# Gate and up products of the last feed-forward as pairs of 64-row products

## The chip, the cores and the metric

The kernel runs on one core of one Trainium2 chip. The metric is the device time of one execution in microseconds (us), from two runs and one more execution that the hardware profiler recorded. Engines are named as in the profile: PE multiplies matrices (PEld is its weight load), DVE, ACT and POOL do elementwise work, SP issues the transfers between the chip's main memory and on-chip memory. Products land in PSUM, in eight banks of 128 partitions by 512 numbers.

## The reference

Two layers over 512 tokens of width 1024. Each layer has a mixer, an attention into 256 memory tokens and a feed-forward with a gate; each of the three is added to its input and normalised. The change is in the feed-forward of the second layer:

```python
FFN_HIDDEN = 2816
def post_norm(h, sub, g, b):
    return layer_norm(DEEPNORM_ALPHA * h.astype(jnp.float32) + sub.astype(jnp.float32), g, b).astype(h.dtype)
...
def swiglu(h, wg, wu, wd):
    return (jax.nn.silu(h @ wg) * (h @ wu)) @ wd
...
        h = post_norm(h, memory_cross_attention(h, mem, xq_w[layer], xk_w[layer], xv_w[layer], xo_w[layer]),
                      ln_x_g[layer], ln_x_b[layer])
        h = post_norm(h, swiglu(h, ffn_wg[layer], ffn_wu[layer], ffn_wd[layer]),
                      ln_ffn_g[layer], ln_ffn_b[layer])
```

## The kernel before

**Numbers in two parts.** Every float32 operand of a large product is split into `hi` (rounded to the format fp32r) and `lo` (the rest, also fp32r). `mm3` replaces one product by three that add up in one bank: hi by hi, hi by lo, lo by hi. An fp32r product of 128 rows, 128 weight columns and 512 moving columns is one PE instruction with one weight load.

**Weights.** `weights` loads a block of 512 KB into a `raw` buffer (two of them), ACT copies it to `hi`, DVE subtracts to get `lo` (four buffers each). Its priority is put 200 places ahead of its users, so loads run early. One block feeds 24 products of 512 columns.

**Order.** Nothing is issued directly. `Order.add` records every operation with the tiles it reads and writes. `Order.order` then plays the program through with a cost for each operation and gives each engine its sequence: the ready operation with the lowest program number goes first, if its buffers can be had. `together` records several products as one operation, so that nothing comes between them; they are issued from line 437, all else from line 439. On the chip each engine follows its sequence strictly.

**The feed-forward** (`ffn`). The hidden width of 2816 is done in two parts, 12 and 10 column blocks of 128 (`FFN_PARTS` counts pairs of them). In each part the gate and up products come first, with the hidden unit on the partitions and the 512 tokens on the moving side: for two blocks of 128 at a time, four banks (gate and up, two blocks), eight steps of 128 input features, three products each. `sink` turns a gate bank and an up bank into one hidden tile: tanh on ACT, two DVE operations, and the split into hi and lo. Then `gemm_tok` multiplies by `wd`, with the tokens on the partitions, in two halves of 512 output columns: four banks, one for each token tile of 128. All but the last eight feature steps are done for the four token tiles together, the last eight token tile by token tile, so that a token tile's end can be worked on while the next is multiplied.

**The input of the feed-forward** is `self.hT`, the normalised tokens turned to features on the partitions, in four tiles (`big_1839` to `big_1842` below, two feature steps each). The attention's output projection before it ends token tile by token tile; `norm_half` normalises a token tile on DVE, `block_to_feat` has PE turn 128 by 128 squares (products with `ident`), and `split` writes the hi part by ACT and the lo part by DVE. The first pair of column blocks (`early`) is done in two halves of 256 tokens, so that its first half needs two of the four token tiles only.

Of the kernel before, what the change touches and what calls it, by code (L numbers as in the profile page):

```python
# [12 lines left out]
AF = mybir.ActivationFunctionType  # L13
OP = mybir.AluOpType
AX = mybir.AxisListType

P = 128
# [443 lines left out]
class Trunk:  # L461
# [755 lines left out]
    def ffn(self, layer, after, fill=iter(())):  # L1217
        a = self.a
        V, A = self.o.V, self.o.A
        wg, wu, wd = a["ffn_wg"][layer], a["ffn_wu"][layer], a["ffn_wd"][layer]  # L1220
        _, _, hact, _ = self.feat_view(self.hT)
        g, b = self.norm_rows("ln_ffn_g", "ln_ffn_b", layer)
        for part, (b0, b1) in enumerate(FFN_PARTS):
            nm = (b1 - b0) * 2
            _, hat, _, htok = self.feat_view([self.big() for _ in range(nm // 2)])

            def sink(m, pg, pu):
                th, sg = self.t2(), self.t2()
                A.activation(th, pg, AF.Tanh, scale=0.5)
                V.scalar_tensor_tensor(sg, th, 1.0, pg, op0=OP.add, op1=OP.mult)  # L1230
                V.tensor_tensor(sg, sg, pu, op=OP.mult)
                self.split(hat(m)[:, 0], hat(m)[:, 1], sg)

            for cb in range(b0, b1):
                pss = [self.bank() for _ in range(4)]
                early = cb == 0
                ws = {}
                for hs in ([slice(0, S // 2), slice(S // 2, S)] if early else [slice(0, S)]):
                    for kh in range(2):
                        for n, w in enumerate((wg, wu)):  # L1240
                            if (kh, n) not in ws:
                                ws[kh, n] = self.weights(w, kh * 4, 4, cb * 256, 256)
                            hi, lo = ws[kh, n]
                            for k in range(4):
                                x = hact(kh * 4 + k)
                                for m in range(2):
                                    cs = slice(m * P, (m + 1) * P)
                                    self.mm3(pss[n * 2 + m][:, hs], (hi[:, k, cs], lo[:, k, cs]), (x[0][:, hs], x[1][:, hs]),
                                             kh == 0 and k == 0, kh == 1 and k == 3)
                for m in range(2):  # L1250
                    sink((cb - b0) * 2 + m, pss[m], pss[2 + m])
                next(fill, None)
            last = part == len(FFN_PARTS) - 1
            for half in range(2):
                rs = self.residual_sinks(half, 2 * ALPHA if part == 0 else 1.0, 4 * LN_EPS, g, b, last, after)
                self.gemm_tok(wd, b0 * 2, nm, half * 512, htok, NT, rs, tail=TAIL)
# [458 lines left out]
```

## Time and profile before

| | |
|---|---|
| median of 2 runs | 1542.75 us (1540.59 and 1544.91) |
| profiled execution | 1543.56 us, span of its instructions 1541.8 us |
| PE busy | 1508.7 us of the span, 8220 products |
| DVE, ACT busy | 984.9 us, 552.5 us |
| mean granted PE clock | 0.995 of 2.4 GHz |
| transfers | 184.01 MB, mean 119 GB/s |

The span runs from the first to the last instruction of the execution; the profiled execution took 1.8 us more than its span. A PE instruction's recorded duration is longer than its turn, since products are pipelined: the turn is read from the start of one to the start of the next.

### The profile page before, as it was taken

To read this page: it belongs to the slowest core of one execution; us is meant where nothing else is said; L and a number is where in the kernel's file an instruction comes from. 1 tells how busy PE (TensorE), PEld (TensorE's weight loads), DVE (VectorE), ACT (ScalarE), POOL (GpSimd) and SP (SyncE) were. 2 spreads that over 40 slices of the span, in tenths; PEclk is the share of its full clock that TensorE was granted. 3 is DMA by queue.
4 is the path that set the end of the run, shared out by engine and by line. 5 is a ranking of instruction groups with operands and counts; after the bars stand their busy time and mean duration, and the time that the engine had idled before them with its cause. 6 is when DMAs were issued, how large, how long until landed. Compare 5 with 4: busy or idle time off the path is not lost.

```text
span 1541.8 us, 21120 instructions
## 1 busy us (share of the span) xinstructions
PE 1508.7 (98%) x8220; PEld 1268.3 (82%) x8220; DVE 984.9 (64%) x1880; ACT 552.5 (36%) x1008; POOL 57.0 (4%) x97
## 2 busy tenths in 40 slices
PE   7999899999999999999999899999999999999998
PEld 5888788689889887888888898888889888888886
DVE  6986576697557888626845899647557444234436
ACT  5533346544523354324341333323423222122311
POOL 1100000010100000010000000000000000000000
PEclk9999999999999999999999999999999999999999
DMA  6424134235223355445562652333212333233322
GB/s 201 115 57 123 47 119 137 64 98 163 62 76 116 110 192 176 150 165 174 186 220 76 245 191 86 128 110 121 65 57 82 109 99 102 85 110 96 96 69 96
DMA packets 125396, 184.01 MB, mean 119 GB/s; under 512 B 14128, under 2 KB 84656, under 8 KB 121200
## 3 DMA queue, kind: packets, MB, share of 16 engines
q1 hardware_dynamic: 125296, 182.66, 37.6%
q8 instruction: 65, 1.06, 0.3%
q14 instruction: 35, 0.29, 0.1%
HBM read 162.45 MB, written 20.19 MB: 118 GB/s over the span
## 4 chain that ended last, share of the span: by engine, by line
PE 88%; DVE 7%; DMA 2%; ACT 1%; issue 1%; SPq 0%; POOL 0%; DVEq 0%; ACTq 0%; POOLq 0%
PE ps L439 86%; DVE t L439 4%; DVE big L439 2%; PE ps L437 2%; DVE lo L439 1%; DMA raw<-in_hyb_w_in_dram 1%; DVE tiny L439 0%; DMA big<-s5m 0%; ACT big L439 0%; DMA raw<-in_xo_w_dram 0%; ACT hi L439 0%; ACT t L439 0%; DMA posi<-in_pos_t_dram 0%; SPq L439 0%; ACT L439 0%
## 5 line engine op out<-in xcount | busy, mean ns | idle before, releaser
L439 PE MATMUL ps<-big,hi 128*128 128x512 f32 (+1 forms) x2368 | 649.5, 360 | 6.1 <-ACT hi L439 4.5
L439 PE MATMUL ps<-hi,big 128*128 128x512 f32 x1728 | 548.2, 394 | 0.7 <-ACT big L439 0.4
L439 PEld LDWEIGHTS ps<-big,hi 128*128 128x128 f32 x2368 | 420.7, 190 | 72.4 <-ACT hi L439 4.7
L439 ACT ACTIVATE hi<-raw 128x1024 fp32r<-128x1024 f32 (+2 forms) x252 | 263.5, 1046 | 513.7 <-PE ps L439 355.7
L439 DVE TENSOR_TENSOR lo<-raw,hi 128x1024 fp32r<-128x1024 f32 (+2 forms) x252 | 303.4, 1205 | 224.8 <-ACT hi L439 221.4
L439 PE MATMUL ps<-big,lo 128*128 128x512 f32 (+1 forms) x1184 | 423.7, 359 | 2.5 <-DVE lo L439 2.5
L439 PEld LDWEIGHTS ps<-hi,big 128*128 128x128 f32 x1728 | 322.6, 188 | 66.4 <-DVE big L439 0.9
L439 PE MATMUL ps<-lo,big 128*128 128x512 f32 x864 | 338.3, 393 | 1.0 <-DVE lo L439 1.0
L439 PEld LDWEIGHTS ps<-big,lo 128*128 128x128 f32 x1184 | 224.6, 190 | 34.5 <-DVE lo L439 2.9
L439 PEld LDWEIGHTS ps<-lo,big 128*128 128x128 f32 x864 | 162.4, 188 | 35.5 <-DVE lo L439 2.2
L439 ACT ACTIVATE big<-ps 128x256 fp32r<-128x256 f32 (+2 forms) x188 | 89.4, 508 | 211.1 <-PE ps L439 202.0
L439 ACT ACTIVATE t<-ps 128x512 f32<-128x512 f32 (+6 forms) x147 | 68.8, 485 | 147.7 <-PE ps L439 139.0
L439 DVE TENSOR_TENSOR big<-ps,big 128x256 fp32r<-128x256 f32 (+1 forms) x152 | 77.6, 541 | 56.9 <-ACT big L439 54.7
L439 DVE SCALAR_TENSOR_TENSOR big<-big,ps 128x512 f32<-128x512 f32 x56 | 38.4, 685 | 86.7 <-PE ps L439 86.7
L439 DVE SCALAR_TENSOR_TENSOR t<-t,ps 128x512 f32<-128x512 f32 x72 | 49.0, 682 | 68.5 <-ACT t L439 49.8
L439 ACT ACTIVATE big<-t 32x128 f32<-32x128 f32 (+2 forms) x148 | 64.9, 455 | 24.3 <-DVE t L439 19.9
L439 DVE SCALAR_TENSOR_TENSOR big<-big,tiny,t 128x512 f32<-128x512 f32 x96 | 66.6, 745 | 0.0
L439 PE MATMUL ps<-ident,t 128*128 128x128 f32 x344 | 62.7, 275 | 3.4 <-ACT t L439 1.8
L439 POOL TENSOR_TENSOR tiny<-tiny,mhalf 128x1 f32<-128x1 f32 (+1 forms) x28 | 23.1, 825 | 962.3 <-DVE tiny L439 953.6
L439 PEld LDWEIGHTS ps<-ident,t 128*128 128x128 f32 x344 | 42.5, 140 | 15.6 <-ACT t L439 5.1
L439 PE MATMUL ps<-big,big 128*128 128x256 f32 (+2 forms) x328 | 54.9, 314 | 0.0
L439 PEld LDWEIGHTS ps<-big,big 128*128 128x128 f32 x328 | 47.8, 190 | 5.0
(145 smaller groups left out, 929.4 us busy)
## 6 DMA issues: line engine op xcount, KB each, us to landing
raw<-in_ffn_wg_dram SPq DMA_DIRECT2D x44, 512.0 KB, 3.8
raw<-in_ffn_wu_dram SPq DMA_DIRECT2D x44, 512.0 KB, 3.6
raw<-in_ffn_wd_dram SPq DMA_DIRECT2D x44, 512.0 KB, 4.1
s5m<-big SPq DMA_DIRECT2D x16, 1024.0 KB, 4.2
big<-s5m SPq DMA_DIRECT2D x16, 1024.0 KB, 6.3
raw<-in_hyb_w_in_dram SPq DMA_DIRECT2D x26, 512.0 KB, 3.8
raw<-in_xk_w_dram SPq DMA_DIRECT2D x16, 512.0 KB, 3.6
raw<-in_xv_w_dram SPq DMA_DIRECT2D x16, 512.0 KB, 4.1
```

Of the source, the lines that this page charges most:

```text
L437: op.inst = getattr(self.eng[e], f)(*a, **k)
L439: op.inst = getattr(self.eng[e], fn)(*args, **kw)
```

## The change

In the second layer the gate and up products take one column block of 128 at a time. Each product of 128 rows becomes two of 64 rows, one in each half of the rows, recorded `together`, and each half adds up in a bank of its own. Behind them ACT copies the first bank of gate to a scratch tile and DVE adds the second bank to it; likewise for up; the two sums go to `sink`. A weight block now holds all eight feature steps of one column block (128 columns, in runs of 512 bytes) where it held four steps of two column blocks (256 columns, 1024 bytes). The number of blocks stays 44. The branch for `early` is no longer taken in this layer.

```diff
+            if layer:
+                for m in range(nm):
+                    pss = [[self.bank() for _ in range(2)] for _ in range(2)]
+                    for n, w in enumerate((wg, wu)):
+                        hi, lo = self.weights(w, 0, 8, (b0 * 2 + m) * P, P)
+                        for k in range(8):
+                            x = hact(k)
+                            for i, (l, r) in enumerate(((hi, x[0]), (hi, x[1]), (lo, x[0]))):
+                                self.o.together(0.227, [
+                                    ((pss[n][u], l[u * 64:(u + 1) * 64, k], r[u * 64:(u + 1) * 64]),
+                                     dict(start=k == 0 and i == 0, stop=k == 7 and i == 2)) for u in range(2)])
+                    sums = []
+                    for n in range(2):
+                        z = self.t2()
+                        A.activation(z, pss[n][0], AF.Copy)
+                        V.tensor_tensor(z, pss[n][1], z, op=OP.add)
+                        sums.append(z)
+                    sink(m, *sums)
-            for cb in range(b0, b1):
+            for cb in range(b0, b1) if not layer else ():
```

PE where the attention's output projection (`ps_1870` is its last bank) goes over into the feed-forward; `ps_1893` takes the turned squares of the last token tile. Before:

```order
L439 MATMUL ps_1870<-hi_1881,big_1758 128x512
L439 MATMUL ps_1905<-big_1839,hi_1910 128x256 x2
L439 MATMUL ps_1905<-big_1839,lo_1911 128x256
...
L439 MATMUL ps_1908<-big_1842,hi_1919 128x256 x2
L439 MATMUL ps_1908<-big_1842,lo_1920 128x256
L439 MATMUL ps_1893<-ident_72,big_1674 128x128 x4
L439 MATMUL ps_1894<-ident_72,big_1674 128x128 x4
```

Between the first and the last of these 256-column products stand 96 of them in all, with three groups of turned squares among them. After the change, the same place:

```order
L439 MATMUL ps_1870<-hi_1881,big_1758 128x512
L439 MATMUL ps_1888<-ident_72,big_1673 128x128 x4
L439 MATMUL ps_1890<-ident_72,big_1674 128x128 x4
L439 MATMUL ps_1891<-ident_72,big_1674 128x128 x4
L439 MATMUL ps_1893<-ident_72,big_1674 128x128 x4
L437 MATMUL ps_1905<-big_1839,hi_1910 128x512
L437 MATMUL ps_1906<-big_1839,hi_1910 128x512
L437 MATMUL ps_1907<-big_1839,hi_1913 128x512
L437 MATMUL ps_1908<-big_1839,hi_1913 128x512
L437 MATMUL ps_1919<-big_1839,hi_1924 128x512
L437 MATMUL ps_1920<-big_1839,hi_1924 128x512
```

The 96 products are gone from here: PE has the turned squares alone between the projection and the first pair, which stands behind `ps_1893`. The two products of a pair follow each other in two banks.

DVE at the same place, the last token tile (`tiny_1892`): the operations with `t_1766` and `t_1767` are the first of the two of its normalisation, those with `t_1768` and `t_1769` the second. Before:

```order
L439 SCALAR_TENSOR_TENSOR big_1674<-big_1674,tiny_1892,t_1766_1843 128x512
L439 SCALAR_TENSOR_TENSOR big_1674<-big_1674,tiny_1892,t_1767_1844 128x512
L439 TENSOR_TENSOR big_1841<-ps_1891,big_1841 128x2x128
L439 TENSOR_TENSOR big_1842<-ps_1891,big_1842 128x2x128
L439 SCALAR_TENSOR_TENSOR big_1674<-big_1674,tiny_1892,t_1768_1845 128x512
L439 SCALAR_TENSOR_TENSOR big_1674<-big_1674,tiny_1892,t_1769_1846 128x512
L439 TENSOR_TENSOR big_1839<-ps_1893,big_1839 128x2x128
```

After:

```order
L439 SCALAR_TENSOR_TENSOR big_1674<-big_1674,tiny_1892,t_1766_1843 128x512
L439 TENSOR_TENSOR big_1839<-ps_1890,big_1839 128x2x128
L439 TENSOR_TENSOR big_1840<-ps_1890,big_1840 128x2x128
L439 SCALAR_TENSOR_TENSOR big_1674<-big_1674,tiny_1892,t_1768_1845 128x512
L439 TENSOR_TENSOR big_1841<-ps_1891,big_1841 128x2x128
L439 TENSOR_TENSOR big_1842<-ps_1891,big_1842 128x2x128
L439 SCALAR_TENSOR_TENSOR big_1674<-big_1674,tiny_1892,t_1767_1844 128x512
L439 TENSOR_TENSOR big_1839<-ps_1893,big_1839 128x2x128
```

The operation with `t_1768`, which ends the first half of the last token tile, has moved ahead of the two on `ps_1891` and of the one with `t_1767`.

## Rows read from the trace of the kernel before

**Rows 1.** Part 1 of the page: busy time, share, instructions.

```profile
PE 1508.7 (98%) x8220; PEld 1268.3 (82%) x8220; DVE 984.9 (64%) x1880; ACT 552.5 (36%) x1008; POOL 57.0 (4%) x97
```

**Rows 2.** The chain that ended last, its end: start, us, engine, tile, count.

```profile
1154.51 29.87 PE ps L439 x189
1184.46 349.73 PE ps L439 x1588
1534.22 0.70 DVE big L439
```

**Rows 3.** Timeline of PE in the last gate and up products: start, us, operation.

```profile
1287.86 0.61 PE L439 MATMUL ps<-big,hi 128*128 128x512 f32 x2
...
1299.42 0.61 PE L439 MATMUL ps<-big,hi 128*128 128x512 f32 x2
```

**Rows 4.** Timeline of all engines at 1300 us, products and weight loads.

```profile
1300.10 0.61 PE L439 MATMUL ps<-big,hi 128*128 128x512 f32 x2
...
1300.33 0.19 PEld L439 LDWEIGHTS ps<-big,lo 128*128 128x128 f32 x1
```

**Rows 5.** Timeline in the first layer's window attention, plain float32, 64-row halves.

```profile
286.53 1.99 PE L437 MATMUL ps<-big,big 64*128 64x512 f32 x8
287.07 0.19 PEld L437 LDWEIGHTS ps<-big,big 64*128 64x128 f32 x2 [0.23 <-issue]
...
287.50 0.19 PEld L437 LDWEIGHTS ps<-big,big 64*128 64x128 f32 x2 [0.24 <-issue]
```

**Rows 6.** Timeline of PE around the first 64-row products.

```profile
226.49 0.39 PE L439 MATMUL ps<-hi,big 128*128 128x512 f32 x1
226.80 0.72 PE L437 MATMUL ps<-big,big 64*128 64x128 f32 x8
227.45 0.50 PE L439 MATMUL ps<-big,hi 128*128 128x256 f32 x2
```

**Rows 7.** Timeline of PE, plain float32 products on all 128 rows.

```profile
862.47 1.95 PE L439 MATMUL ps<-t,big 128*128 128x128 f32 x16
```

**Rows 8.** Timeline of PE where the last feed-forward begins.

```profile
1170.82 0.40 PE L439 MATMUL ps<-big,hi 128*128 128x256 f32 x2
...
1182.07 0.28 PE L439 MATMUL ps<-big,lo 128*128 128x256 f32 x1
...
1182.43 0.28 PE L439 MATMUL ps<-big,lo 128*128 128x256 f32 x1
...
1183.71 1.38 PE L439 MATMUL ps<-ident,big 128*128 128x128 f32 x8
```

**Rows 9.** Timeline of DVE and ACT at the same place.

```profile
1182.24 0.75 DVE L439 TENSOR_TENSOR big<-ps,big 128x256 fp32r<-128x256 f32 x2
1182.91 1.41 DVE L439 SCALAR_TENSOR_TENSOR big<-big,tiny,t 128x512 f32<-128x512 f32 x2
...
1184.40 1.38 ACT L439 ACTIVATE big<-ps 128x256 fp32r<-128x256 f32 x4 [2.55 <-PE ps L439]
...
1185.10 1.48 DVE L439 TENSOR_TENSOR big<-ps,big 128x256 fp32r<-128x256 f32 x4 [0.78 <-PE ps L439]
```

**Rows 10.** A pause; stretches: length, PE, PEld, DVE, ACT, POOL busy, clock, DMA, GB/s.

```profile
872.65 0.58 PE L439 MATMUL ps<-big,lo 128*128 128x256 f32 x1 [2.06 <-DVE lo L439]
...
872.20:875.60 3.40, 2.94 (x14) 2.95 (x14) 3.40 (x6) 0.00 (x0) 0.00 (x0) 0.51 0.53 166
...
1184.40:1534.20 349.80, 349.72 (x1588) 291.18 (x1588) 143.64 (x172) 89.51 (x110) 2.87 (x3) 1.00 0.31 94
```

**Rows 11.** Groups by form from 1190 to 1530 us: busy, mean ns, idle before.

```profile
L439 DVE TENSOR_TENSOR lo<-raw,hi 128x1024 fp32r<-128x1024 f32 x62 | 76.0, 1225 | 110.4 <-ACT hi L439 110.1
...
L439 DVE TENSOR_TENSOR t<-t,ps 128x512 f32<-128x512 f32 x22 | 15.0, 688 | 21.2 <-PE ps L439 21.2
...
L439 ACT ACTIVATE t<-ps 128x512 f32<-128x512 f32 x22 | 12.9, 590 | 40.2 <-PE ps L439 40.2
```

**Rows 12.** Part 6 of the page: transfers, KB each, median us from issue to landing.

```profile
raw<-in_ffn_wg_dram SPq DMA_DIRECT2D x44, 512.0 KB, 3.8
```

## The prediction

> **What bounds the kernel now.** I read the page's busy shares first. PE is busy for 98% of the span, DVE for 64% and ACT for 36% [rows 1]. Since a busy PE may still be waiting inside a stage, the chain that ended last comes next: from 1184.46 us to 1534.2 us, which is the whole last feed-forward but its start, the chain is PE alone, and only DVE's last normalisation follows [rows 2]. So a PE turn that is added or saved there moves the end one for one, and work on DVE or ACT costs nothing while it stays hidden.
>
> What is one turn? In the gate and up products the timeline shows a product starting at 1287.86 us and the one 51 places later at 1299.42 us [rows 3]: 11.56 / 51 = 0.2267 us. At 2.4 GHz and one column a clock 512 columns take 0.2133 us, so 0.0133 us of each turn is fixed. The 256-column products bear this out: three of them take 1182.43 - 1182.07 = 0.36 us [rows 8], 0.120 us each, of which the columns are 0.1067 and again 0.0133 is left. The weight load isn't the cause in any plain way: the load of 1300.33 us begins when the product before it does (1300.10 + 0.61 - 0.39 = 1300.32) and ends at 1300.52 us, before its own product's turn [rows 4].
>
> **The pairs.** Removed are 960 products of 512 columns and 192 of 256; 22 column blocks x 2 weights x 8 steps x 3 = 1056 pairs take their place. A pair does the arithmetic of one product on all rows. The question is its turn. The trace has pairs in the two row halves, in plain float32, in the first layer's window attention: eight 64-row products of 512 columns take 1.99 us [rows 5]. In plain float32 a column takes two clocks (below), 0.427 us for 512, so one after the other they would need 8 x 0.427 = 3.4 us. They run side by side: two loads start together at 287.07 us and the next two at 287.50 us [rows 5], a turn of 0.43 us for a pair, which is the columns and about 0.003 us. At 128 columns eight take 0.72 us [rows 6], while full-row products of that shape take a turn of (1.95 - 0.28) / 15 = 0.111 us [rows 7], two clocks a column and 0.005 us (the last of them lasts some 0.28 us, as the single products of [rows 8] do); four pairs at that turn would take 0.61 us with the first one's start missing. So in plain float32 a pair costs what one full product costs, no less and no more.
>
> No row shows such a pair in fp32r at one column a clock. I bound its turn by rows: below by the columns with the small fixed part of the float32 pairs, 0.2133 + 0.003 = 0.216 us; above, among cases where the halves run side by side, by the fixed part paid once for each of the two products, 0.2133 + 2 x 0.0133 = 0.240 us. I take 0.2267 us, the turn of the full product in the same format, because the one comparison that the trace allows, 128 columns in float32, found pair and product alike. Against before that is nothing for the 960 products, and for the first two blocks 96 x 0.2267 = 21.8 us in place of 192 x 0.120 = 23.0 us.
>
> **The start of the stage is where I expect the cost.** Before, PE goes from the attention's projection straight into 96 products of 256 columns that need two token tiles only, and is busy with them from 1170.82 us until the last token tile's squares come at 1183.71 us [rows 8]: 96 x 0.120 = 11.5 us of useful work. After the change the first pair reads all 512 tokens, and in PE's sequence it stands behind `ps_1893`, so PE has nothing but turned squares for that time; no other product is put there. When can it begin? Before, the second operations of the last token tile start at 1182.91 us and the squares at 1183.71 [rows 9, 8]. DVE's new sequence does the first of them ahead of two splits (0.75 us) and of one more normalisation operation (0.7 us): squares at about 1182.3 us. From the squares' start to DVE's first lo part it took 1185.10 + 0.37 - 1183.71 = 1.76 us [rows 9, 8], which gives 1184.0 us; three pairs that need hi parts alone (0.7 us) go ahead of it. So I count full work from 1183.5 us, between 1182.9 and 1184.5 us, the time at which the chain takes PE up before.
>
> From there: 1056 x 0.2267 = 239.4 us of pairs, 528 x 0.2267 = 119.7 us of down products (22 steps x 2 halves x 4 token tiles x 3), 0.4 us for the last four squares. PE ends at 1183.5 + 359.5 = 1543.0 us, against 1534.2 us before: **+8.8 us**. The same sum for before, from 1184.46: 96 x 0.120 + 1488 x 0.2267 + 0.4 = 349.2 us, where the chain has 349.73.
>
> **The clock.** After a pause of 2.06 us PE takes up work at 872.65 us and the granted clock of 872.2 to 875.6 us is 0.51, which is the 1.2 GHz level [rows 10]. The new pause is some 12 us, with four groups of squares in it. I take the same price, 3.4 us at half pace, **+1.7 us**; it is between 0 and 2.
>
> **Changes between 64-row and 128-row products.** Into the first 64-row products the start-to-start time is 226.80 - 226.49 = 0.31 us instead of 0.227 [rows 6], 0.08 us more. There are six such changes (around `ps_1894`, and between pairs and down products): **+0.6 us** at 0.1 each.
>
> **What is hidden.** The sums add 44 copies on ACT at 0.59 us (26 us) and 44 additions on DVE at 0.69 us (30 us) [rows 11]. From 1184.4 to 1534.2 us DVE is busy for 143.64 and ACT for 89.51 of 349.80 us [rows 10], so both stay at half. A block's first bank pair is read out while 24 pairs (5.4 us) of the other weight run, and its banks are wanted again only after another block (10.9 us). At the end of a part the last hidden tile comes about 2.6 us later (two copies, two additions); the down products have 48 and 24 products (10.9 and 5.4 us) ready that don't read the last eight steps, and begin those with the oldest. Without this cover each part would lose up to 2.6 us. The weight blocks come in twice as many, half as long runs. Now a block lands 3.8 us after its issue [rows 12], and a `raw` buffer is used anew every second block, 10.9 us: twice the landing time, 7.6 us, would still leave 3.3 us for the copy and the subtraction (1.23 us [rows 11]). SP's sequence has the same number of issues in the same order of gate and up; nothing is queued behind a new wait there.
>
> Sum: 8.8 + 1.7 + 0.6 = 11.1 us. The profiled execution took 1543.56 us (span 1541.8 and 1.8 around it), so it would take 1554.7; the median of the runs is 0.8 us lower, and **1554 us** is the forecast.
>
> **Rivals.** *The halves take turns* (the slower side). If in fp32r the two row halves can't both deliver a column in each clock, a pair costs two full turns, and 1056 x 0.2267 = 239 us come on top: 1793 us. For it: no row shows 64-row fp32r products, and the float32 pairs deliver only one column from each half in two clocks. Against it: nothing in the float32 pairs shows one half waiting for the other; their loads start together. It decides early: with 11 us already lost, the pair needs only (31 - 11) / 1056 = 0.019 us more than 0.2267 to be 2% slower.
>
> *The fixed part goes* (the side of no loss). If the 0.0133 us is a hand-over from one set of weights to the next, which two halves can hide from each other, a pair takes 0.216 us, 1056 x 0.0107 = 11.3 us come back, and the time is 1543 us; with no fixed part at all 1540 us. For it: the float32 pairs of 512 columns lose only 0.003 us. Against it: full products in float32 lose little too (0.005), so the 0.0133 seems to belong to fp32r and not to the rows. Below 0.216 us the change would begin to pay. The Trainium skill (TensorE: Matmul & The Clock Gate, Part 3, The mechanism) speaks for this rival: a weight load overlaps a running product only where the row groups differ. By that rule the products before would pay for each load, and the pairs would not, which gives this rival's time. The trace of before disagrees, since the load of [rows 4], on all rows, lies inside a running product; so the rule gets no more weight here than the float32 rows give.
>
> *The fixed part is paid twice*: 0.240 us, 1056 x 0.0133 = 14 us more, 1568 us. For it: twice as many loads and products go through PE's sequence. Against it: the float32 pairs don't pay twice.
>
> That the change isn't what it says is ruled out by the sequence: the two products of a pair stand next to each other, in two banks.
>
> **How the numbers follow.** Forecast (pair as one product, 1550 to 1558 by the bounds of start and clock): 0.52. Fixed part gone or partly gone (1540 to 1550): 0.2. Paid twice or partly (1558 to 1568): 0.13. Taking turns: 0.12. Something unseen, such as late weights: 0.03. The range from 1541 to 1568 us leaves out the halves taking turns, the unseen, and the outer edge of the second case. A measurement of this kernel can tell about 2%, 31 us, from no change: faster than 1512 us nothing here reaches (0.01); slower than 1574 us are turns taken and half of the unseen (0.14); the rest, 0.85, is within 2%.
>
> **What would show it.** In the profile after: (1) loads of 64 rows in twos, with 0.227 us from one two to the next, between 1184 and 1543 us; 0.216, 0.240 or 0.453 decide for a rival. (2) PE idle, but for squares, from 1171 us to about 1183, with the granted clock at half for the first 3 us of pairs. (3) The chain still PE alone from there to the last down product. (4) DVE and ACT about 30 and 26 us busier. The prediction is wrong if the turn of a pair isn't that of a product, or if a load or a bank is waited for in mid-stage.

## The result, and the profile after

The changed kernel takes **1556.51 us** (median of two runs, 1556.31 and 1556.7) against 1542.75 us before. The ratio is 1.0088, with a 95% interval from 1.006 to 1.0115: 13.8 us slower, which is within 2% and yet more than the measurement is uncertain. The forecast was 1554 us, from 1541 to 1568. The profiled execution took 1556.7 us (span 1554.9), 13.1 us more than the profiled one of before.

The page's busy shares, which answer to [rows 1], have 960 more products and weight loads, 29 us more on DVE and 27 us more on ACT:

```profile
PE 1513.7 (97%) x9180; PEld 1274.1 (82%) x9180; DVE 1014.3 (65%) x1924; ACT 579.5 (37%) x1052; POOL 58.1 (4%) x97
```

The end of the chain that ended last (start, us, engine, tile, line, count) answers to [rows 2]. L437 is the helper that records the pairs, L439 that of everything else:

```profile
1184.46 3.36 PE ps L437 x14
1187.81 1.04 PE ps L439 x4
1188.86 129.27 PE ps L437 x1134
1318.12 65.53 PE ps L439 x288
1383.65 109.05 PE ps L437 x960
1492.69 54.66 PE ps L439 x240
1547.38 0.70 DVE big L439
```

As before, PE alone sets the time from 1184.46 us on, with no wait for a load, a bank or a sum. The chain's PE part is 362.9 us long where it was 349.73, and it begins at the same time.

The timeline of PE where the last feed-forward begins (start, us, operation, and in brackets the idle time before it and what ended that) answers to [rows 8]:

```profile
1171.80 0.40 PE L439 MATMUL ps<-hi,big 128*128 128x512 f32 x1
1172.72 0.66 PE L439 MATMUL ps<-ident,big 128*128 128x128 f32 x4 [0.52 <-DVE big L439]
1179.37 1.11 PE L439 MATMUL ps<-ident,big 128*128 128x128 f32 x4 [6.00 <-DVE big L439]
...
1182.90 1.09 PE L439 MATMUL ps<-ident,big 128*128 128x128 f32 x4 [0.96 <-DVE big L439]
1184.46 2.08 PE L437 MATMUL ps<-big,hi 64*128 64x512 f32 x8 [0.47 <-ACT big L439]
...
1195.55 0.40 PE L437 MATMUL ps<-big,lo 64*128 64x512 f32 x2
...
1198.27 0.40 PE L437 MATMUL ps<-big,lo 64*128 64x512 f32 x2
```

The first line is the last product of the projection. Where 96 products stood before, PE has four groups of turned squares, with waits of 0.52, 6.00, 0.34 (the group left out) and 0.96 us ahead of them, and one of 0.47 us ahead of the first pair. The last two lines are 12 pairs apart: 2.72 / 12 = 0.2267 us for a pair, to the last digit the turn of a full product in [rows 3].

Stretches of the same place (length, then busy time and count of PE, PEld, DVE, ACT and POOL, granted clock, DMA share, GB/s); the last line answers to the last of [rows 10]:

```profile
1171.00:1183.00 12.00, 4.19 (x19) 2.61 (x18) 11.84 (x24) 4.09 (x8) 1.52 (x2) 0.68 0.60 175
1184.40:1188.90 4.50, 4.44 (x20) 3.00 (x20) 1.41 (x3) 0.28 (x3) 0.00 (x0) 0.50 0.02 4
1184.40:1547.20 362.80, 362.74 (x2644) 306.20 (x2644) 174.26 (x217) 115.97 (x154) 2.87 (x3) 0.99 0.30 91
```

While PE pauses, DVE is busy for 11.84 of 12.00 us: the pause is the time of DVE's normalisation and splits. Two of its operations there, 1.18 us from 1175.68 and 1.22 us from 1177.43, make lo parts of weight blocks, which these squares don't need; whether the pause is shorter without them was not tried. The first 4.5 us of pairs run at a granted clock of 0.50, the 1.2 GHz level; over the whole stage it is 0.99.

**One measure for all kernels.** Up to the projection PE's program is the same in all of them, and yet its last product starts at 1170.59 us before and anywhere from 1168.33 to 1173.40 us in the profiled executions of the others. So I read the stage by itself: from the start of the projection's last product to the start of the last down product. Before it is 363.20 us, after 1546.95 - 1171.80 = 375.15 us: **+11.95 us** of the 13.1 that separate the two profiled executions lie in the stage. The other 1.2 us lie ahead of it (1171.80 - 1170.59), inside the scatter just named. The trace of after shows where they arise. After the pause of [rows 10] PE takes up work at 872.40 us, 0.25 us earlier than before, and then its granted clock stays at half for some 7 us, where it was 3.4 us before:

```profile
871.40:878.40 7.00, 6.00 (x28) 6.00 (x29) 7.00 (x11) 1.06 (x1) 0.10 (x1) 0.51 0.60 193
```

PE's program is the same there, so this difference is not the change's.

| kernel | median, us | ratio to before (95%) | stage, us | against before, us |
|---|---|---|---|---|
| before | 1542.75 | | 363.20 | |
| after | 1556.51 | 1.0088 (1.006 to 1.0115) | 375.15 | +11.95 |
| early blocks back (e1) | 1545.55 | 1.0009 (0.9999 to 1.0019) | 364.14 | +0.94 |
| before without the early products (e2) | 1554.17 | 1.0058 (1.004 to 1.0076) | 373.70 | +10.50 |
| after's order, full rows (e3) | 1555.69 | 1.0067 (1.0048 to 1.0087) | 374.47 | +11.27 |
| after without the sums (e4) | 1554.83 | 1.0064 (1.0042 to 1.0086) | 374.98 | +11.78 |
| pause filled with products (e6) | 1554.49 | 1.0064 (1.0041 to 1.0087) | 374.15 | +10.95 |
| one block early, as pairs (e7) | 1551.04 | 1.0044 (1.0028 to 1.006) | 370.43 | +7.23 |
| three and three (e9), one run | 1556.39 | | 375.50 | +12.30 |
| halves apart (e5), one run | 1926.53 | | 745.03 | |
| halves apart, pause filled (e8), one run | 1727.93 | | 548.36 | |

The kernel before took 1544.36 us beside e1 to e4, 1544.43 us beside e5 to e7 and 1544.72 us beside e8 and e9; each ratio is against those. Against these values after's 1556.51 us is some 12.1 us slower, near the stage's 11.95; the 1542.75 us of two runs lie 1.6 us lower.

### The profile page after: what moved, and what is told of

The parts are those of the page before. It is cut to its first block, busy times and chain, and to the rows that moved or that the text cites. A ratio compares the mean times of both kernels' runs of the same rounds, so it can differ in the third digit from the quotient of the medians.

```text
span 1554.9 us, 23108 instructions
## 1 busy us (share of the span) xinstructions
PE 1513.7 (97%) x9180; PEld 1274.1 (82%) x9180; DVE 1014.3 (65%) x1924; ACT 579.5 (37%) x1052; POOL 58.1 (4%) x97
## 3 DMA queue, kind: packets, MB, share of 16 engines
q8 instruction: 72, 1.18, 0.3%
## 4 chain that ended last, share of the span: by engine, by line
PE 87%; DVE 8%; DMA 2%; issue 1%; ACT 1%; SPq 0%; POOL 0%; DVEq 0%; ACTq 0%; POOLq 0%
PE ps L439 70%; PE ps L437 17%; DVE t L439 4%; DVE big L439 2%; DVE lo L439 1%; DMA raw<-in_hyb_w_in_dram 1%; DVE tiny L439 1%; ACT big L439 0%; DMA big<-s5m 0%; DMA raw<-in_xo_w_dram 0%; SPq L439 0%; ACT hi L439 0%; ACT t L439 0%; DMA posi<-in_pos_t_dram 0%; ACT L439 0%
## 5 line engine op out<-in xcount | busy, mean ns | idle before, releaser
L439 PE MATMUL ps<-hi,big 128*128 128x512 f32 x1728 | 549.0, 395 | 0.8 <-ACT big L439 0.4
L439 DVE TENSOR_TENSOR lo<-raw,hi 128x1024 fp32r<-128x1024 f32 (+2 forms) x252 | 303.3, 1204 | 226.9 <-ACT hi L439 223.6
L439 PE MATMUL ps<-big,hi 128*128 128x512 f32 (+1 forms) x1600 | 429.9, 356 | 6.0 <-ACT hi L439 4.4
L439 ACT ACTIVATE hi<-raw 128x1024 fp32r<-128x1024 f32 (+2 forms) x252 | 263.4, 1045 | 457.9 <-PE ps L439 273.5
L439 PEld LDWEIGHTS ps<-hi,big 128*128 128x128 f32 x1728 | 322.9, 188 | 67.4 <-issue 1.4
L439 PE MATMUL ps<-lo,big 128*128 128x512 f32 x864 | 338.7, 394 | 1.0 <-DVE lo L439 1.0
L439 PEld LDWEIGHTS ps<-big,hi 128*128 128x128 f32 x1600 | 281.7, 192 | 46.9 <-ACT hi L439 4.4
L439 PE MATMUL ps<-big,lo 128*128 128x512 f32 (+1 forms) x800 | 282.0, 355 | 2.5 <-DVE lo L439 2.5
L437 PE MATMUL ps<-big,hi 64*128 64x512 f32 x1408 | 221.1, 389 | 0.5 <-ACT big L439 0.5
L439 PEld LDWEIGHTS ps<-lo,big 128*128 128x128 f32 x864 | 162.5, 188 | 35.3 <-DVE lo L439 2.1
L439 PEld LDWEIGHTS ps<-big,lo 128*128 128x128 f32 x800 | 153.0, 192 | 21.9 <-DVE lo L439 2.9
L439 ACT ACTIVATE big<-ps 128x256 fp32r<-128x256 f32 (+2 forms) x188 | 89.4, 508 | 215.2 <-PE ps L439 205.7
L437 PEld LDWEIGHTS ps<-big,hi 64*128 64x128 f32 x1408 | 137.7, 186 | 23.7 <-ACT big L439 0.9
L437 PE MATMUL ps<-big,lo 64*128 64x512 f32 x704 | 140.1, 388 | 0.0
L439 ACT ACTIVATE t<-ps 128x512 f32<-128x512 f32 (+6 forms) x169 | 81.3, 495 | 108.8 <-PE ps L439 99.9
L439 DVE TENSOR_TENSOR big<-ps,big 128x256 fp32r<-128x256 f32 (+1 forms) x152 | 77.5, 540 | 59.8 <-ACT big L439 58.3
L439 DVE SCALAR_TENSOR_TENSOR big<-big,ps 128x512 f32<-128x512 f32 x56 | 38.3, 685 | 87.8 <-PE ps L439 87.8
L439 ACT ACTIVATE big<-t 32x128 f32<-32x128 f32 (+2 forms) x148 | 66.2, 458 | 68.8 <-DVE t L439 64.5
L437 PEld LDWEIGHTS ps<-big,lo 64*128 64x128 f32 x704 | 68.9, 185 | 11.6 <-issue 0.3
L439 DVE SCALAR_TENSOR_TENSOR big<-big,tiny,t 128x512 f32<-128x512 f32 x96 | 66.6, 744 | 0.0
L439 PE MATMUL ps<-ident,t 128*128 128x128 f32 x344 | 62.8, 275 | 3.4 <-ACT t L439 1.8
L439 DVE TENSOR_TENSOR big<-t,big 128x512 fp32r<-128x512 f32 (+1 forms) x68 | 45.0, 681 | 26.3 <-ACT big L439 26.2
```

The costliest lines, as they stand in the source:

```text
L437: op.inst = getattr(self.eng[e], f)(*a, **k)
L439: op.inst = getattr(self.eng[e], fn)(*args, **kw)
```

## The experiments

My theory was that a pair costs what a product costs, so that the loss is the early work at the start of the stage, with the low clock and the changes between row modes on top. The rivals were that the pairs themselves cost something (in their turn, their loads, their banks or their sums), and that the two halves hide something from each other which another order would lose.

### e1: the early blocks back, all others as pairs

The first two column blocks are done again by the old loop, with their 256-column products on all rows; the other 20 stay pairs, in a loop that now stands behind the old one. This diff is against the kernel after, as are all that follow but e2's.

```diff
-            for cb in range(b0, b1) if not layer else ():
+            for cb in range(b0, b1) if not layer else range(1 - part):
...
-                for m in range(nm):
+                for m in range(2 if part == 0 else 0, nm):
```

> The first two column blocks go back to whole-row products in two token halves, as before the change; the other 20 blocks stay pairs with sums. Theory (a pair costs one product, all of the loss is the lost early start and the clock): PE is busy again from 1171 us, no low clock at 1184 to 1188 us, 960 pairs at 0.227 us, and the time is that of before within 2 us, 1541 to 1546 us. Rival (the pairs, their sums, or the changes between row modes cost the 13 us): 20 of 22 blocks still pay, about 1554 us.

Measured: 1545.55 us, 1.0009 times before. The chain, from the last projection on (the line x100 is the rest of the first two blocks):

```profile
1157.32 29.87 PE ps L439 x189
1187.28 12.41 PE ps L439 x100
1199.68 109.02 PE ps L437 x960
...
```

PE goes straight from the projection into early products again: the first line has the length that it has in [rows 2], and no low clock follows:

```profile
1173.00:1190.00 17.00, 16.90 (x137) 16.24 (x136) 14.74 (x30) 5.30 (x12) 1.52 (x2) 1.00 0.41 123
```

With 20 of 22 blocks as pairs the stage is 0.94 us longer than before, while the loss of the full change is 11.95. So the pairs, with their loads, banks and sums, are not where the time went.

### e2: before, with the early products taken away

The other direction: full-row products throughout, and only the early order switched off in the last feed-forward. The diff is against the kernel before.

```diff
-                early = cb == 0
+                early = cb == 0 and not layer
```

> The kernel before, with the token halves of the first two column blocks taken away in the second layer and nothing else: whole-row products of 512 columns, no pairs, no sums. Theory: PE waits from 1171 to about 1184 us here too, low clock at the restart, 1555 to 1557 us, as the change. Rival (pairs cost): 1543 to 1546 us.

Measured: 1554.17 us, ratio 1.0058, somewhat under the range given; the stage is 10.50 us longer than before. No pair is in this kernel, and most of the loss is. Its stretches:

```profile
1171.00:1184.00 13.00, 4.93 (x21) 3.00 (x19) 12.68 (x26) 4.20 (x9) 1.52 (x2) 0.75 0.56 161
1184.00:1188.00 4.00, 3.78 (x12) 3.00 (x13) 1.41 (x3) 0.45 (x2) 0.00 (x0) 0.53 0.01 4
1184.20:1187.70 3.50, 3.48 (x9) 2.69 (x10) 1.41 (x3) 0.25 (x1) 0.00 (x0) 0.50 0.02 5
```

The pause is that of the changed kernel, and a low clock follows it here too, for 3.5 us (the last line). Both come from what PE has to do there, not from 64-row products.

### e3: the order and blocks of after, on all rows

Every pair becomes one 128-row product in one bank; there are no sums.

```diff
-                    pss = [[self.bank() for _ in range(2)] for _ in range(2)]
+                    pss = [self.bank() for _ in range(2)]
...
+                            self.mm3(pss[n], (hi[:, k], lo[:, k]), hact(k), k == 0, k == 7)
+                    sink(m, *pss)
```

> The changed kernel's order and weight blocks (one column block of 128, eight steps), but each pair put back into one product of 128 rows in one bank, without the sums. Theory: 1555 to 1557 us, since 1056 products at 0.227 us stand where 1056 pairs at 0.227 us stood. Rival (pairs or sums cost some of the 13 us): below 1552 us; rival (pairs save a part of the fixed 0.013 us): above 1558 us.

Measured: 1555.69 us, ratio 1.0067; the stage is 11.27 us longer than before and 0.68 us shorter than after. The line of the chain that answers to the second of [rows 2]:

```profile
1185.85 362.22 PE ps L439 x1588
```

The 1588 products and squares are 1056 + 528 + 4, and at 0.2267 us for a product they would need 359.5 us. From 1185.85 to 1191.0 us the granted clock is 0.50, and half of those 5.15 us is 2.6. So full rows and pairs differ by 0.7 us in all, on the side of the full rows, although their low clock lasted longer than after's 4.4 us.

### e4: after, without the sums

The second bank of each pair goes to `sink` alone; the first bank's half of every gate and up value is left out.

```diff
-                    sums = []
-                    for n in range(2):
-                        z = self.t2()
-                        A.activation(z, pss[n][0], AF.Copy)
-                        V.tensor_tensor(z, pss[n][1], z, op=OP.add)
-                        sums.append(z)
+                    sums = [p[1] for p in pss]
```

> The changed kernel without the copies and additions: the hidden tiles are made from the second half's bank alone, so the first half's products are computed and not used. Theory (sums hidden on DVE and ACT): the same time as the change, 1555 to 1557 us, DVE and ACT 30 and 26 us less busy. Rival (the sums hold up banks or the step from gate and up to down): 1 to 5 us faster.

Measured: 1554.83 us, ratio 1.0064, with a stage 0.17 us shorter than after. The median is a little under the range given and, 1.7 us below after's, in that of the rival; but in the profiled execution the stage, where the rival would have to show, has only the 0.17. The page's busy shares show the work gone, 30.5 us from DVE and 28 us from ACT:

```profile
PE 1511.1 (97%) x9180; PEld 1277.3 (82%) x9180; DVE 983.8 (63%) x1880; ACT 551.8 (36%) x1008; POOL 58.1 (4%) x97
```

So the sums lie beside PE's work: 30 us of DVE are worth 0.2 us at the end.

### e5: the two halves one after the other

All 24 products of the upper half of the rows, then all 24 of the lower; work, banks and sums as in the changed kernel. This was to give a price to the rival in which the halves take turns.

```diff
-                        for k in range(8):
-                            x = hact(k)
...
+                        for u in range(2):
+                            us = slice(u * 64, (u + 1) * 64)
+                            for k in range(8):
+                                x = hact(k)
+                                self.mm3(pss[n][u], (hi[us, k], lo[us, k]), (x[0][us], x[1][us]), k == 0, k == 7)
```

> The changed kernel with the partners pulled apart: per weight block first all 24 products of the upper 64 rows, then all 24 of the lower ones, into the same two banks, with the same sums. Theory (a 64-row product takes a full turn, and only a neighbour in the other half runs beside it): 2112 turns of 0.227 us, 239 us more than the change, about 1795 us. Rival (a 64-row product takes less than a full turn, or the halves overlap however they are ordered): under 1700 us.

Measured: 1926.53 us, 131 us more than I had expected. The sign was right and the size was not. Stretches late in part 1, at its end, and in part 2:

```profile
1490.00:1590.00 100.00, 100.00 (x279) 79.47 (x279) 15.49 (x20) 13.55 (x18) 0.00 (x0) 0.50 0.08 27
1590.00:1690.00 100.00, 100.00 (x411) 81.09 (x410) 27.12 (x29) 17.94 (x20) 0.00 (x0) 0.90 0.26 79
1690.00:1790.00 100.00, 100.00 (x513) 82.77 (x512) 30.58 (x38) 24.19 (x32) 0.00 (x0) 1.00 0.18 53
```

PE is busy for 100% in all three, but from 1177.5 to 1611 us the granted clock is 0.50. In part 2 the same products run at 1.00. The timeline of PE shows where it rose:

```profile
1605.49 0.62 PE L439 MATMUL ps<-big,lo 64*128 64x512 f32 x1
1606.04 0.79 PE L439 MATMUL ps<-hi,big 128*128 128x512 f32 x1
...
1610.47 0.62 PE L439 MATMUL ps<-lo,big 128*128 128x512 f32 x1
...
1611.40 0.40 PE L439 MATMUL ps<-lo,big 128*128 128x512 f32 x1
```

The first line is the last lone 64-row product of part 1, the second the first down product on all rows. Some 5 us later products last 0.40 us where they lasted 0.62. So the clock, low since the pause, stayed low through some 420 us of mostly lone 64-row products (1186.29 to 1606.04 us), and rose under whole rows. This is one execution. A second thing is in the counts: at the full clock 513 products in 100 us are 0.195 us each, not 0.2267. Over a run of 24 that is 24 x 0.2267 - 24 x 0.195 = 0.76 us less, or 3.4 turns: at each border some three products of one half run beside those of the other. At the low clock it is the same picture: 24 x 0.427 - 24 x 100 / 279 = 1.6 us, 3.8 turns of 0.427.

### e6: the pause filled

Whether the clock after the pause costs what I took was still argued only. Here 44 products on all rows, which nobody reads, stand in the pause.

```diff
+                        if part == m == n == 0:
+                            spare = self.bank()
+                            self.o.bias = 30
+                            for _ in range(22):
+                                self.o.together(0.454, [((spare, hi[:, 0], hi[:, :4]), dict(start=True, stop=True))] * 2)
+                            self.o.bias = 0
```

> The changed kernel with 44 products of weights by weights put into PE's pause ahead of the first pair; they go to a spare bank and nothing reads them. Theory (part of the loss is the half clock after the pause): the granted clock stays near 1.00 from 1171 to 1190 us, the turned squares take 0.66 instead of 1.1 us, and the time falls by 2 to 4 us against the change, to 1552 to 1554 us, with the lost 10 us of early work still lost. Rival (the clock costs nothing, or the fill delays the squares as much as it saves): 1556 to 1558 us.

Measured: 1554.49 us, ratio 1.0064. The stretches of the place:

```profile
1171.00:1183.00 12.00, 11.80 (x58) 9.43 (x56) 11.63 (x24) 3.99 (x8) 2.60 (x2) 1.00 0.58 170
1183.00:1187.00 4.00, 3.15 (x24) 2.23 (x26) 2.79 (x7) 1.26 (x4) 0.00 (x0) 1.00 0.00 0
```

The clock stays at 1.00, and from the first pair to the last down product it takes 1545.14 - 1185.01 = 360.13 us where after takes 1546.95 - 1184.46 = 362.49. Of the 2.36 us, 0.4 are the last four squares, which here come ahead of the first pair; the other 2.0 us are about what the clock gives back. The time gained is small because the first pair itself comes later, 14.02 us after the last projection product instead of 12.66:

```profile
1183.85 1.23 PE L439 MATMUL ps<-ident,big 128*128 128x128 f32 x8 [1.05 <-DVE big L439]
1185.01 1.18 PE L437 MATMUL ps<-big,hi 64*128 64x512 f32 x6
```

The squares of the last token tile come as one group of eight, after DVE: with the fillers DVE's sequence is another, and the normalisation that they wait for starts at 1182.96 us, 11.97 us after the last projection product, where in after it is 10.21. So the stage is only 1.0 us shorter than after, and the median a little above the range given.

### e7: the first block early, as pairs of 256 columns

If the lost start is the cause, a part of it should come back without any full-row product. The first block's pairs are split into token halves, so that the first 48 pairs need two token tiles only.

```diff
+                    early = part == 0 and m == 0
...
+                    for hs, n in [(hs, n) for hs in ([slice(0, S // 2), slice(S // 2, S)] if early else [slice(0, S)])
+                                  for n in range(2)]:
...
-                                    ((pss[n][u], l[u * 64:(u + 1) * 64, k], r[u * 64:(u + 1) * 64]),
+                                    ((pss[n][u][:, hs], l[u * 64:(u + 1) * 64, k], r[u * 64:(u + 1) * 64, hs]),
```

> The changed kernel with the first column block alone in two token halves, still as pairs (96 pairs of 256 columns in place of 48 of 512). Theory: 48 pairs x 0.120 us = 5.8 us of work fit into the pause, half of what was lost, less 0.6 us for the shorter products, and the clock falls for a shorter time: 5 to 7 us faster than the change, 1549 to 1551 us; a pair of 256 columns takes a turn of 0.120 us. Rival (the loss is not early work, but the pairs): 1555 us or more.

Measured: 1551.04 us, ratio 1.0044, at the upper edge of the range given; the stage is 4.7 us shorter than after. The timeline of PE in the former pause:

```profile
1178.46 0.40 PE L437 MATMUL ps<-big,hi 64*128 64x256 f32 x4
...
1179.18 0.40 PE L437 MATMUL ps<-big,hi 64*128 64x256 f32 x4
...
1180.14 1.38 PE L439 MATMUL ps<-ident,big 128*128 128x128 f32 x8
1185.31 1.97 PE L439 MATMUL ps<-ident,big 128*128 128x128 f32 x8 [3.79 <-DVE big L439]
```

The two upper lines are six pairs apart, 0.72 / 6 = 0.120 us each: a pair of 256 columns costs what a 256-column product does [rows 8]. The 48 pairs are 48 x 0.120 = 5.8 us of work. PE still pauses for 3.79 us, and a low clock follows, to 1191.0 us, which takes part of the gain back. Two blocks, as before, are what fills the whole pause (e1).

### e8: halves apart, with the pause filled

This tells whether e5's extra 131 us are the clock: e5's order, with the fillers of e6.

```diff
+                            for _ in range(22):
+                                self.o.together(0.454, [((spare, hi[:, 0], hi[:, :4]), dict(start=True, stop=True))] * 2)
+                            self.o.bias = 0
+                        for u in range(2):
+                            us = slice(u * 64, (u + 1) * 64)
```

> The partners pulled apart as before (24 products of the upper half, then 24 of the lower), with PE's pause ahead of them filled by 44 unread products, so that the stage begins at full clock. Theory (the last run's extra 131 us came from the clock, which was low when the 64-row products began and didn't rise under them; a clock that is up stays up): granted clock 1.00 through the stage, 2112 products at the mean of 0.195 us that the second part of the last run had at full clock, 172 us more than with pairs, about 1727 us. Rival (64-row products one at a time pull the clock down by themselves): low clock again, over 1850 us.

Measured: 1727.93 us, 199 us less than e5 with 44 products more. Two stretches of part 1 and part 2:

```profile
1190.00:1290.00 100.00, 100.00 (x512) 82.76 (x512) 30.07 (x38) 24.40 (x33) 0.00 (x0) 1.00 0.18 53
1590.00:1690.00 100.00, 100.00 (x491) 82.49 (x490) 31.47 (x40) 21.81 (x28) 0.00 (x0) 1.00 0.17 53
```

With no pause ahead of it, the clock is at 1.00 from the first lone product on and stays there under the very products under which it did not rise in e5. It also prices the halves in turn: 2112 products at 0.195 us are 412 us in place of 239, 173 more, and the stages differ by 548.36 - 375.15 = 173.2. The timeline of PE at one border shows the overlap that e5's counts only implied:

```profile
1253.98 0.83 PE L439 MATMUL ps<-big,hi 64*128 64x512 f32 x4
1254.54 0.49 PE L439 MATMUL ps<-big,lo 64*128 64x512 f32 x2
1254.78 0.62 PE L439 MATMUL ps<-big,hi 64*128 64x512 f32 x2
```

The first six of these products, three of each half, take 1254.78 - 1253.98 = 0.80 us from the first's start to the seventh's; one after the other they would take 6 x 0.2267 = 1.36.

### e9: three products of one half, then three of the other

```diff
-                            for i, (l, r) in enumerate(((hi, x[0]), (hi, x[1]), (lo, x[0]))):
-                                self.o.together(0.227, [
...
+                            self.o.together(1.36, [
...
+                                for u in range(2) for i, (l, r) in enumerate(((hi, x[0]), (hi, x[1]), (lo, x[0])))])
```

> The changed kernel with the order inside a step changed: the three products of the upper half, then the three of the lower, in place of three pairs. Theory (each half takes up products some places ahead of the other, as the overlaps at the ends of the runs of 24 suggest): the halves stay side by side, 0.68 us for a step of six, 1556 to 1565 us. Rival (only the next product can run beside the current one): five turns for six products, 352 steps x 2 turns x 0.227 = 160 us more, about 1716 us.

Measured: 1556.39 us, as after. The timeline of PE, 12 pairs apart:

```profile
1300.37 0.42 PE L437 MATMUL ps<-big,lo 64*128 64x512 f32 x2
...
1303.09 0.42 PE L437 MATMUL ps<-big,lo 64*128 64x512 f32 x2
```

Again 2.72 / 12 = 0.2267 us. The halves run side by side although three products of one half stand ahead of the other's in the program, which fits the 3.4 turns of e5. If only two neighbours could overlap, six products would take four turns (the expectation's five leave out the overlap with the next step), 352 x 0.2267 = 80 us more.

No version here beats the kernel before, and nothing in the runs points to one: on all rows and in halves PE sends through the same columns in the same time.

## Why the prediction was right

**What bounds the kernel** was read rightly: a turn on PE moves the end, and work on DVE and ACT does not (e4).

**The pair's turn**, the term on which the forecast hung, is 0.2267 us, the value taken, between bounds of 0.216 and 0.240. With it the three rivals about the turn fall. Halves that take turns would need 0.453 us a pair; one half after the other costs 173 us (e8). The fixed part did not go, and it is not paid twice: at 256 columns it is there as well (0.120 us, e7). The rival that I had placed beside the Trainium skill (TensorE: Matmul & The Clock Gate, Part 3, The mechanism), in which a load overlaps only where row groups differ, would have given 0.216 us: no pair of this kernel shows it.

**The lost early start** was put at +8.8 us, with full work counted from 1183.5 us, which is 12.9 us after the last projection product; the first pair came after 12.66 us, so the term was 0.25 us too large. That it is the cause is shown from both sides: with the early products back 0.94 us of the loss is left (e1), and without them full-row products lose 10.50 us (e2).

**The clock** was put at +1.7 us, between 0 and 2. PE is busy for 4.44 us at 0.50, and half of that is 2.2; with the pause filled the pairs gain about 2.0 (e6). It was under-sized, a little over the upper bound, and it isn't a fixed price: the half clock lasted 3.5 us in e2 and 5.15 in e3 after the same pause. I took a row of 3.4 us after a pause of 2 us as the price after a pause of 12.

**The changes between row modes** were under-sized too: +0.6 us at 0.1 each. The timeline of after, at the border from pairs to down products and at that from down products to pairs:

```profile
1317.72 0.40 PE L437 MATMUL ps<-big,lo 64*128 64x512 f32 x2
1318.05 0.50 PE L439 MATMUL ps<-hi,big 128*128 128x512 f32 x1
1318.39 0.40 PE L439 MATMUL ps<-lo,big 128*128 128x512 f32 x1
...
1383.26 0.39 PE L439 MATMUL ps<-hi,big 128*128 128x512 f32 x1
1383.58 0.73 PE L437 MATMUL ps<-big,hi 64*128 64x512 f32 x4
1384.15 0.40 PE L437 MATMUL ps<-big,lo 64*128 64x512 f32 x2
```

The first product of the new kind starts 0.33 us after the last of the old, 0.10 more than a turn, which is what [rows 6] show and what I took. But the turn after it is long too, 0.34 us. [rows 6] held that part as well: eight products took 0.72 us where I worked out 0.61, and I put the difference down to the start of the first. At the second border it is 0.32 us, and two pairs then take 0.57 where 0.453 would do. So a change at the full clock costs 0.21 us. In e1, with four changes and none of the other costs, 4 x 0.21 = 0.84 of the 0.94 us are accounted for. Three of the six of after lie around turned squares at the half clock, where the trace doesn't show a price for each. What all six cost follows from the kernels without pairs: after's stage is 1.45 us longer than e2's, of which (4.4 - 3.5) / 2 = 0.45 is the clock's, and 0.68 us longer than e3's, although its clock cost some 0.4 less. Either way about 1.0 us is left for the six, 0.4 more than forecast. The Trainium skill (TensorEngine Tiling (Array Packing), Tiling Modes, Key Properties) says that changing the tiling mode drains the engine; the longer steps at the borders fit that, though the trace shows no drain as such, and the 0.21 us is this kernel's price of it.

**The sum** then reads 8.8 - 0.25 + 2.2 + 1.0 = 11.75 us, where the stage shows 11.95. Most of the 0.2 us left is a slip in the 8.8: it lets the changed kernel's last product end after a turn of 0.23 us, while the 1534.2 us of before include all 0.40 us of that product. The profiled execution was forecast at 1554.7 us and took 2.0 more: 0.85 in the stage (11.95 against 11.1), from terms that were too small, and 1.2 ahead of it, where the change does nothing. That share is chance.

**What was to be hidden is hidden.** The sums cost 0.2 us (e4); the page has DVE and ACT busier by 29 and 27 us, against 30 and 26 forecast. The weight blocks land as fast as before, though twice as many runs are asked for. The page's part 6, to be set beside [rows 12]:

```profile
raw<-in_ffn_wg_dram SPq DMA_DIRECT2D x44, 512.0 KB, 3.7
```

**What would show it**: points (1), (3) and (4) came as written. For (1), the weight loads of after, where three twos of 64-row loads take 1301.18 - 1300.50 = 0.68 us:

```profile
1300.50 0.20 PEld L437 LDWEIGHTS ps<-big,lo 64*128 64x128 f32 x2
...
1301.18 0.20 PEld L437 LDWEIGHTS ps<-big,lo 64*128 64x128 f32 x2
```

In (2) the pause lasted to 1184.46 us, of which 1.2 lie ahead of the stage, and the half clock for 4.4 us, against about 1183 and 3.

## What to carry to other kernels

Where the contraction already filled all 128 rows, splitting it into two row halves gained nothing here: a pair sends the same columns in the same turn, and the sums and mode changes come on top. The price of this rewrite lay at the start of its stage. In such a case, look for the work that the old form could begin on part of its input, count what no longer fits into the wait (11.5 us of products here), and add the low clock after the new pause (1.8 to 2.6 us here) and some 0.2 us for each change of row mode. If 64-row products are used, keep the two halves close to each other in the program, and keep PE busy ahead of them.

## What the runs showed of the hardware that was not expected

- The granted clock stayed at the 1.2 GHz level for 433 us, from a pause on and through some 420 us in which 64-row products ran mostly one at a time and kept PE 100% busy (e5, one execution). It rose some 5 us after whole-row products began there, and in the changed kernel 4.4 us after pairs began. Once at the 2.4 GHz level it stayed there under the same lone products (e8, and part 2 of e5).
- The two row halves don't wait for each other in program order. With runs of 24, some 3.4 to 3.8 turns at each border ran beside the other half (e5), and at full clock six products at a border take 0.80 us in place of 1.36 (e8); with threes nothing is lost (e9, 0.2267 us). So that each engine follows its sequence strictly, as I wrote of the kernel before, doesn't hold for PE's row halves. The Trainium skill (TensorE: Matmul & The Clock Gate, Part 3, The mechanism) has matmuls start and end strictly in order. By that rule one product at most would overlap at a border, and three pairs in e9 would take four turns instead of three; both runs disagree.
- What a turn has beyond its columns, 0.0133 us, belongs to the product or pair as such: it is the same on all rows and in halves, at 512 columns (0.2267 us) and at 256 (0.120 us).
- Two halves that write one bank were not tried.
